# Weights-stationary products of a hybrid decoder layer: a pair of 512 and 256 columns, or three of 256 into one sum

## Chip, cores and metric

The kernel runs on one core of one Trainium2 chip. The metric is the device time of one execution in microseconds (us). Most of the computation is matrix products on TensorE (PE); VectorE (DVE), ScalarE (ACT) and GpSimd (POOL) prepare weights and finish results; SyncE (SP) issues the transfers of the weights. In the profile PEld is TensorE's loading of a stationary operand, which has rows of its own.

## What is computed

One decoder layer in float32 on 256 tokens of width 2048: a combined input projection into attention heads and a causal pooling mixer, an output projection into the residual, then a gated MLP of width 5632 with a causal convolution of width 3.

```python
D_MODEL, SEQ, D_FF, POOL_WINDOWS = 2048, 256, 5632, (2, 4, 8, 16)

def multiscale_pool(p, pool_w, pool_scale):     # 4 groups of 256 channels
    ...
        mixed = (cg[:, 1:] - cg[:, start]) / count - pf[:, :, sl]
        outs.append(jnp.einsum('bsc,cd->bsd', mixed.astype(p.dtype), pool_w[g]))
    ...

def conv_ffn(h, w_up, conv_w, conv_b, w_down):
    u = h @ w_up
    ...                                          # y = conv_b + sum of conv_w[i] * u shifted
    gate, val = jnp.split(y, 2, axis=-1)
    return (jax.nn.silu(gate) * val) @ w_down

def reference(x, ...):
    h = rms_norm(x, attn_norm_g[l])
    q, k, v, p = jnp.split(h @ w_in[l], ...)
    a = moba_attention(rms_norm(q), rms_norm(k), v, rel_bias)
    m = multiscale_pool(p, pool_w[l], pool_scale[l])
    x = x + jnp.concatenate([a, m], axis=-1) @ w_out[l]
    x = x + conv_ffn(rms_norm(x, ffn_norm_g[l]), w_up[l], conv_w[l], conv_b[l], w_down[l])
```

## The kernel before

**Split numbers.** To multiply float32 numbers with single-pass products, every operand is kept as two parts, a rounded one and the remainder. Weights arrive as `raw` chunks of 128x2048; ACT writes the rounded part `wh` (L115), DVE the remainder `wl` (L116). Activations (`xh`, `cat`, `x2h`, `hid`) are stored with both parts side by side, `[128, 16, 2, 256]`: for each of 16 slices of the inner dimension 256 tokens of the rounded part (index 0), then 256 of the remainder (index 1). A product is the sum of three terms: wh with part 0, wh with part 1, wl with part 0.

**Two kinds of product.** For q, k and v (`tok_half`, L145) the activations are stationary and 512 columns of weights move. For everything else (`feat_half`) a 128x128 block of weights is stationary and the tokens move: the pooling input, the output projection, the MLP's gate and value, the MLP's down projection. There `feat_mm` takes for each slice a **pair**: one product of wh with all 512 columns (both parts, L152), and one of wl with 256 columns (L154) that adds to the second half of the same PSUM tile. So a PSUM tile holds two halves, and `add_halves` (L379 on ACT, L380 on DVE) joins them in SBUF before anything else is done. The last block of the down projection and the pooling weights use `feat_sum` (L161) instead: three products of 256 columns into one sum, without halves to be joined.

**Blocks and queues.** A step is half a chunk of weights, 16 products in pairs for two output tiles; four steps (two chunks) make a block of 256 output channels in the MLP's up projection. Gate and value blocks alternate, in three groups of 8, 8 and 6, each followed by eight down blocks. After a block's last product, `gate` and `value` call `conv`: join the halves, times the row's scale into `u` (L561), three taps of the convolution into `y` (L566 on ACT, L567 and L569 on DVE), and for a value block the gate (L583) and the split into `hid` (L584, L585). `add_to_x2` does the same for the residual (L515). The order on each engine is that of the code: at every second step the next chunk but one is split, and its ACT and DVE instructions stand behind those of the block that ended before. There are three buffers for the two parts of weights, two for the PSUM tile `acc`.

**Pooling.** `pool_window` scales a group's channels by the row's scale into `pa[0]` (L386), adds shifted copies (L390), and leaves `pst` (L392, L393), on POOL for groups 3, 2 and 1 and on DVE for group 0; `pool_mixed` splits `pst` into `cat` (L399, L400).

**Places.** `WOFF` sets at which element each part of weights begins in a tile that is 64 elements longer than needed. The tiles of weights begin 32 bytes past a multiple of 256, those of the activations 128 bytes past one. From chunk 24 on (all weights-stationary chunks), wh begins at element 8, that is at 64 past a multiple of 256 and so 192 past the activations' place, counted round 256; wl begins at element 28, at 144 and so 16 past it. All slices and blocks that a product reads begin at multiples of 512 or 1024 bytes from there, so these distances hold for every one.

Of the kernel before, what the change touches and what calls it, by code (L numbers as in the profile page):

```python
# [23 lines left out]
F32 = mybir.dt.float32  # L24
F32R = mybir.dt.float32r
AF = mybir.ActivationFunctionType
OP = mybir.AluOpType
AX = mybir.AxisListType

P = 128  # L30
D = 2048
S = 256
# [16 lines left out]
NPAR = C_CB + 2 * NF  # L49
OK = (0, 4, 12, 8)  # L50
TOK_CHUNKS = 24
WOFF = ((24, 24), (8, 28))
THIRDS = ((0, 8), (8, 16), (16, 22))


# [16 lines left out]
def layer(ctx: ExitStack, tc: tile.TileContext, xT, wts, par, relT, ident_d, onehot_d, icnt_d, out):  # L72
    nc = tc.nc
# [3 lines left out]
    mm = ctx.enter_context(tc.tile_pool(name="mm", bufs=2, space=bass.MemoryType.PSUM))  # L77
# [5 lines left out]
    def acc(name):  # L83
        return mm.tile([P, 2, 512], F32, name=name, tag="acc")
# [4 lines left out]
    def small(name):  # L89
        return sm.tile([P, 512], F32, name=name, tag="small")  # L90
# [3 lines left out]
    def col(c):  # L94
        return pv[:, c:c + 1]
# [11 lines left out]
    def split_piece(c, lo, n):  # L107

        if c not in wparts:
            offs = WOFF[0 if c < TOK_CHUNKS else 1]  # L110
            wparts[c] = tuple(wpool.tile([P, CH + 64], F32R, name=w, tag=w)[:, o:o + CH]
# [15 lines left out]
    def half(u):  # L127

        parts = wparts[u // 2] if u % 2 == 0 else wparts.pop(u // 2)
        return tuple(w[:, (u % 2) * HALF:(u % 2 + 1) * HALF] for w in parts)  # L130
# [15 lines left out]
                                     start=(first and k == 0 and n == 0),  # L146
                                     stop=(last and k == 1 and n == 2))

    def feat_mm(ps, wh, wl, act, ks, first, last):

        for n, (ws, k) in enumerate(ks):
            nc.tensor.matmul(ps, wh[:, ws], act[:, k, :, :],  # L152
                             start=(first and n == 0), stop=False, skip_group_check=True)
            nc.tensor.matmul(ps[:, S:], wl[:, ws], act[:, k, 0, :], start=False,  # L154
                             stop=(last and n == len(ks) - 1), skip_group_check=True)

    def feat_sum(ps, wh, wl, act, ks, first, last):

        for n, (ws, k) in enumerate(ks):
            for i, (w, a) in enumerate(((wh, 0), (wh, 1), (wl, 0))):  # L160
                nc.tensor.matmul(ps, w[:, ws], act[:, k, a, :], start=(first and n == 0 and i == 0),  # L161
                                 stop=(last and n == len(ks) - 1 and i == 2))

    def feat_half(u, act, k0, ps, first, last, mm=feat_mm):
        wh, wl = half(u)
        for m in range(2):
            mm(ps[m], wh, wl, act,
               [(slice(k * 256 + m * P, k * 256 + (m + 1) * P), k0 + k) for k in range(4)],
               first, last)


    xh = keep.tile([P, KT, 2, S], F32R, name="xh", tag="h")
# [20 lines left out]
    ps = small("ps_start")  # L193
# [74 lines left out]
    rrow = keep.tile([P, S], F32, name="rrow", tag="rrow")  # L268
# [103 lines left out]
    PAD = 16  # L372
    pa = [early.tile([P, 2, PAD + S], F32, name=f"pa{i}") for i in range(3)]
    for t_ in pa:
        nc.gpsimd.memset(t_[:, :, :PAD], 0.0)

    def add_halves(dst, ps):

        nc.scalar.activation(dst, ps[:, :, S:], AF.Copy)  # L379
        nc.vector.tensor_tensor(dst, ps[:, :, :S], dst, op=OP.add)  # L380

    def pool_window(ps, g):
        s = early.tile([P, 2, S], F32, name="pst", tag=("sq", "hn")[g % 2])
        eng = nc.gpsimd if g else nc.vector
        add_halves(s, ps)
        eng.tensor_tensor(pa[0][:, :, PAD:], s, rrow[:, None, :].to_broadcast([P, 2, S]), op=OP.mult)  # L386
        cur, d, i = pa[0], 1, 1
        while d < WINDOWS[g]:
            nxt = pa[i]
            eng.tensor_tensor(nxt[:, :, PAD:], cur[:, :, PAD:], cur[:, :, PAD - d:PAD + S - d], op=OP.add)  # L390
            cur, d, i = nxt, 2 * d, 3 - i
        eng.tensor_tensor(s, cur[:, :, PAD:], icnt[:, g:g + 1, :].to_broadcast([P, 2, S]), op=OP.mult)  # L392
        eng.tensor_tensor(s, s, pa[0][:, :, PAD:], op=OP.subtract)  # L393
        st["win", g] = s
# [46 lines left out]
    def feat_block(act, ks, post, final=False):  # L441
        box, runs = {}, []
        for i, k0 in enumerate(ks):
            def run(u, i=i, k0=k0):
                if i == 0:
                    box["acc"] = None if final else acc("ps_feat")
                    box["ps"] = [small("ps_feat")[:, :S] if final else box["acc"][:, m, :] for m in range(2)]
                feat_half(u, act(), k0, box["ps"], i == 0, i == len(ks) - 1, feat_sum if final else feat_mm)
                if i == len(ks) - 1:
                    post(box["ps"] if final else box["acc"])  # L450
            runs.append([run])
        return runs
# [12 lines left out]
    for g in (3, 2, 1, 0):  # L465
        steps += feat_block(lambda: xh, XK, lambda ps, g=g: pool_window(ps, g))
        after(len(steps) + (2 if g else 0), lambda g=g: pool_mixed(g))
# [15 lines left out]
    for b in range(2):  # L483
# [4 lines left out]
        for j in range(4):  # L488
            h, u = 4 * b + j, at + 2 * j
# [8 lines left out]
    late = {}  # L498
# [11 lines left out]
            nc.gpsimd.memset(u[:, :, :2], 0.0)  # L510

    def add_to_x2(ps, g):
        x2, s = late["x2"][:, 2 * g:2 * g + 2, :], late["pool"].tile([P, 2, S], F32, name="fs", tag="fs", bufs=2)
        add_halves(s, ps)
        nc.vector.tensor_tensor(x2, s, x2, op=OP.add)  # L515
        return x2

    def residual(ps, g):
        x2 = add_to_x2(ps, g)
        if g == 0:  # L520
            nc.scalar.activation(late["sq"], x2, AF.Square)
            return
        s = late["pool"].tile([P, 2, S], F32, name="xs", tag="y0", bufs=2)
        nc.scalar.activation(s, x2, AF.Square)
        nc.gpsimd.tensor_tensor(late["sq"], late["sq"], s, op=OP.add)
# [30 lines left out]
    def conv(ps, f0_, which):  # L556

        pool, u = late["pool"], late["u"][which]
        s = pool.tile([P, 2, S], F32, name="fs", tag="fs", bufs=2)
        add_halves(s, ps)  # L560
        nc.vector.tensor_tensor(u[:, :, 2:], s, late["rrow"][:, None, :].to_broadcast([P, 2, S]), op=OP.mult)  # L561
        y = pool.tile([P, 2, S], F32, name="y", tag=f"y{which}", bufs=2)
        for m in range(2):
            f = f0_ + m
            cw = [col(C_CW + i * 2 * NF + f) for i in range(3)]
            nc.scalar.activation(y[:, m, :], u[:, m, 2:], AF.Identity, scale=cw[2], bias=col(C_CB + f))  # L566
            nc.vector.scalar_tensor_tensor(y[:, m, :], u[:, m, 1:1 + S], cw[1], y[:, m, :],  # L567
                                           op0=OP.mult, op1=OP.add)
            nc.vector.scalar_tensor_tensor(y[:, m, :], u[:, m, :S], cw[0], y[:, m, :],  # L569
                                           op0=OP.mult, op1=OP.add)  # L570
        return y

    def gate(ps, g):
        y = conv(ps, 2 * g, 0)
        nc.scalar.activation(y, y, AF.Silu)
        late["gate"] = y

    def value(ps, g, j):
        if j == 0:
            late["hid"] = keep.tile([P, KT, 2, S], F32R, name="hid", tag="c")  # L580
        y = conv(ps, NF + 2 * g, 1)
        hid, ks = late["hid"], slice(2 * j, 2 * j + 2)
        nc.vector.tensor_tensor(y, y, late["gate"], op=OP.mult)  # L583
        nc.scalar.activation(hid[:, ks, 0, :], y, AF.Copy)  # L584
        nc.vector.tensor_tensor(hid[:, ks, 1, :], y, hid[:, ks, 0, :].bitcast(F32), op=OP.subtract)  # L585

    def down(ps, g, last, final):
        x2 = late["x2"]
        if final:
            for m in range(2):  # L590
                k = 2 * g + m
                nc.vector.tensor_tensor(x2[:, k, :], ps[m], x2[:, k, :], op=OP.add)
                nc.sync.dma_start(out[:, k, :], x2[:, k, :])
            return
        add_to_x2(ps, g)
        if last:
            nc.sync.dma_start(out[:, 2 * g:2 * g + 2, :], x2[:, 2 * g:2 * g + 2, :])

    for n, (g0, g1) in enumerate(THIRDS):
# [4 lines left out]
        for g in range(D // 256):  # L604
            final = n == 2 and g == D // 256 - 1
            blocks.append(feat_block(lambda: late["hid"], range(0, 2 * (g1 - g0), 4),
                                     lambda ps, g=g, n=n, final=final: down(ps, g, n == 2, final), final))
# [4 lines left out]
    n = len(steps)  # L612
# [77 lines left out]
```

## Time and profile before

| | |
|---|---|
| median of 3 executions | 1046.59 us (1043.42 to 1058.9) |
| the profiled execution | 1045.45 us, its span 1043.3 us |
| PE busy | 1029.2 us, 5786 products |
| DVE, ACT busy | 690.5 us, 514.1 us |
| products as pairs (L152, L154) | 2472 of each |
| products in threes (L161) | 120 |
| joining halves (L379, L380) | 79 each |

The span reaches from the first instruction to the last of the profiled execution; 2.15 us lie around it. PE's rows overlap, since a product's row begins before the one ahead of it has ended; how fast products follow each other is read from the distance of their starts, not from their durations. In the sections below "pace" is that distance.

### The profile page before, as it was taken

Reading aid. Unit: us, or ns where it says so; the run is one execution under the profiler, and the core shown is the slowest. Engines: PE = TensorE matmul, PEld = TensorE weight load, DVE = VectorE, ACT = ScalarE, POOL = GpSimd, SP = SyncE. Lnnn points to the kernel's source line nnn. Section 1 sums busy time; section 2 is a strip of 40 time slices with the busy share of each in tenths; the row PEclk is TensorE's granted clock in tenths of the full one; section 3 lists DMA queues with packets and bytes.
Section 4 is the critical chain, followed back from the end, with each engine's and each line's share of the span. In section 5 each row is a group of like instructions: output and inputs, shape, how many; then the busy total and the mean of one; then the engine's idle time right before and its main releaser. Section 6 shows DMA issues by size and latency. Waiting matters only on the chain.

```text
span 1043.3 us, 13818 instructions
## 1 busy us (share of the span) xinstructions
PE 1029.2 (99%) x5786; PEld 894.1 (86%) x5786; DVE 690.5 (66%) x729; ACT 514.1 (49%) x532; POOL 63.2 (6%) x44
## 2 busy tenths in 40 slices
PE   9999999999999999999999999999999999999998
PEld 7788788888888888888888888888888888888887
DVE  6744667766567777777655677767765557777763
ACT  7534444546465455445433455455453344554541
POOL 0700004611110000000000000000000000000000
PEclk9999999999999999999999999999999999999999
DMA  9767644464644554454645444544565545545561
GB/s 342 271 169 205 226 171 161 152 245 182 225 166 161 190 212 164 185 217 163 239 173 199 186 173 167 211 188 162 206 221 196 184 161 202 203 161 182 218 205 41
DMA packets 31390, 200.42 MB, mean 192 GB/s; under 512 B 3816, under 2 KB 4872, under 8 KB 8544
## 3 DMA queue, kind: packets, MB, share of 16 engines
q1 hardware_dynamic: 30336, 196.92, 51.6%
q0 software_dynamic: 992, 2.63, 1.6%
q8 instruction: 45, 0.74, 0.3%
q14 instruction: 17, 0.14, 0.0%
HBM read 195.86 MB, written 3.67 MB: 191 GB/s over the span
## 4 chain that ended last, share of the span: by engine, by line
PE 55%; DVE 20%; ACT 10%; issue 8%; POOL 4%; DMA 3%; SPq 0%; ACTq 0%; DVEq 0%; POOLq 0%
PE ps_feat L152 31%; PE ps_feat L154 16%; DVE wl L116 8%; ACT wh L115 7%; PE ps_tok L145 6%; DMA raw<-in_wts 3%; DVE y L569 3%; DVE y L567 2%; DVE u L561 2%; DVE fs L380 2%; ACT y L566 2%; POOL xboth L274 1%; POOL pa L390 1%; DVE y L583 1%; PE ps_feat L161 1%
## 5 line engine op out<-in xcount | busy, mean ns | idle before, releaser
L116 DVE TENSOR_TENSOR wl<-raw,wh 128x2048 fp32r<-128x2048 f32 (+2 forms) x189 | 420.7, 2247 | 206.1 <-ACT wh L115 206.0
L152 PE MATMUL ps_feat<-x2h,wh 128*128 128x512 f32 x1408 | 488.8, 393 | 0.0
L154 PE MATMUL ps_feat<-x2h,wl 128*128 128x256 f32 x1408 | 391.9, 278 | 1.3 <-DVE wl L116 0.9
L115 ACT ACTIVATE wh<-raw 128x2048 fp32r<-128x2048 f32 (+2 forms) x189 | 342.9, 1837 | 96.1 <-PE ps_feat L152 58.4
L152 PEld LDWEIGHTS ps_feat<-x2h,wh 128*128 128x128 f32 x1408 | 263.9, 187 | 60.2
L154 PEld LDWEIGHTS ps_feat<-x2h,wl 128*128 128x128 f32 x1408 | 264.4, 188 | 4.8 <-DVE wl L116 4.4
L152 PE MATMUL ps_feat<-hid,wh 128*128 128x512 f32 x680 | 232.4, 390 | 0.0
L154 PE MATMUL ps_feat<-hid,wl 128*128 128x256 f32 x680 | 188.0, 277 | 0.5 <-DVE wl L116 0.5
L152 PEld LDWEIGHTS ps_feat<-hid,wh 128*128 128x128 f32 x680 | 127.6, 188 | 27.3
L154 PEld LDWEIGHTS ps_feat<-hid,wl 128*128 128x128 f32 x680 | 127.7, 188 | 0.8 <-DVE wl L116 0.8
L145 PE MATMUL ps_tok<-wh,xh 128*128 128x512 f32 x384 | 125.3, 402 | 0.5 <-ACT wh L115 0.5
L379 ACT ACTIVATE fs<-ps_feat 128x512 f32<-128x512 f32 x75 | 44.9, 599 | 131.5 <-PE ps_feat L154 131.5
L566 ACT ACTIVATE y<-u,pv 128x256 f32<-128x256 f32 x88 | 48.2, 595 | 116.7 <-DVE u L561 116.7
L145 PEld LDWEIGHTS ps_tok<-wh,xh 128*128 128x128 f32 x384 | 73.9, 192 | 16.5 <-ACT wh L115 0.7
L152 PE MATMUL ps_feat<-cat,wh 128*128 128x512 f32 x256 | 87.2, 389 | 0.0
L380 DVE TENSOR_TENSOR fs<-ps_feat,fs 128x512 f32<-128x512 f32 x75 | 51.5, 686 | 47.1 <-ACT fs L379 47.1
L145 PE MATMUL ps_tok<-wl,xh 128*128 128x512 f32 x192 | 76.4, 398 | 0.0
L154 PE MATMUL ps_feat<-cat,wl 128*128 128x256 f32 x256 | 70.7, 276 | 0.0
L567 DVE SCALAR_TENSOR_TENSOR y<-u,pv,y 128x256 f32<-128x256 f32 x88 | 42.4, 482 | 29.6 <-ACT y L566 29.6
L152 PEld LDWEIGHTS ps_feat<-cat,wh 128*128 128x128 f32 x256 | 48.1, 188 | 10.0
L154 PEld LDWEIGHTS ps_feat<-cat,wl 128*128 128x128 f32 x256 | 48.1, 188 | 0.0
L152 PE MATMUL ps_feat<-xh,wh 128*128 128x512 f32 x128 | 46.2, 403 | 0.0
(112 smaller groups left out, 568.6 us busy)
## 6 DMA issues: line engine op xcount, KB each, us to landing
raw<-in_wts SPq DMA_DIRECT2D x177, 1024.0 KB, 5.0
raw<-in_wts SPq DMA_DIRECT2D x6, 512.0 KB, 8.0
x<-in_xT SPq DMA_DIRECT2D x1, 2048.0 KB, 9.1
out<-x SPq DMA_DIRECT2D x7, 256.0 KB, 2.1
xboth<-in_xT SPq DMA_DIRECT2D x6, 256.0 KB, 7.9
band<-rsb POOLq DMA_DIRECT2D x1, 1536.0 KB, 37.2
raw<-in_wts SPq DMA_DIRECT2D x4, 256.0 KB, 4.1
T<-band POOLq DMA_DIRECT2D x2, 512.0 KB, 7.2
```

The lines of the kernel that those rows point to most:

```text
L115: nc.scalar.activation(wh, w, AF.Copy)
L116: nc.vector.tensor_tensor(wl, w, wh.bitcast(F32), op=OP.subtract)
L145: nc.tensor.matmul(ps[:, t, :], act[:, k0 + k, a, ts], w[:, ws], start=(first and k == 0 and n == 0), stop=(last and k == 1 and n == 2))
L152: nc.tensor.matmul(ps, wh[:, ws], act[:, k, :, :], start=(first and n == 0), stop=False, skip_group_check=True)
L154: nc.tensor.matmul(ps[:, S:], wl[:, ws], act[:, k, 0, :], start=False, stop=(last and n == len(ks) - 1), skip_group_check=True)
L161: nc.tensor.matmul(ps, w[:, ws], act[:, k, a, :], start=(first and n == 0 and i == 0), stop=(last and n == len(ks) - 1 and i == 2))
L379: nc.scalar.activation(dst, ps[:, :, S:], AF.Copy)
L380: nc.vector.tensor_tensor(dst, ps[:, :, :S], dst, op=OP.add)
L561: nc.vector.tensor_tensor(u[:, :, 2:], s, late["rrow"][:, None, :].to_broadcast([P, 2, S]), op=OP.mult)
L566: nc.scalar.activation(y[:, m, :], u[:, m, 2:], AF.Identity, scale=cw[2], bias=col(C_CB + f))
L567: nc.vector.scalar_tensor_tensor(y[:, m, :], u[:, m, 1:1 + S], cw[1], y[:, m, :], op0=OP.mult, op1=OP.add)
L569: nc.vector.scalar_tensor_tensor(y[:, m, :], u[:, m, :S], cw[0], y[:, m, :], op0=OP.mult, op1=OP.add)
```

## The change

Every weights-stationary product uses `feat_sum`; `feat_mm` and `add_halves` go; what used the joined halves reads PSUM directly. wl begins at element 8 like wh, so both are 192 bytes past the activations' place.

```diff
-WOFF = ((24, 24), (8, 28))
+WOFF = ((24, 24), (8, 8))
...
-    def feat_mm(ps, wh, wl, act, ks, first, last):
-        for n, (ws, k) in enumerate(ks):
-            nc.tensor.matmul(ps, wh[:, ws], act[:, k, :, :],
-                             start=(first and n == 0), stop=False, skip_group_check=True)
-            nc.tensor.matmul(ps[:, S:], wl[:, ws], act[:, k, 0, :], start=False,
-                             stop=(last and n == len(ks) - 1), skip_group_check=True)
...
     def feat_sum(ps, wh, wl, act, ks, first, last):
         for n, (ws, k) in enumerate(ks):
             for i, (w, a) in enumerate(((wh, 0), (wh, 1), (wl, 0))):
                 nc.tensor.matmul(ps, w[:, ws], act[:, k, a, :], start=(first and n == 0 and i == 0),
                                  stop=(last and n == len(ks) - 1 and i == 2))
...
-    def add_halves(dst, ps):
-        nc.scalar.activation(dst, ps[:, :, S:], AF.Copy)
-        nc.vector.tensor_tensor(dst, ps[:, :, :S], dst, op=OP.add)
...
     def pool_window(ps, g):
         eng = nc.gpsimd if g else nc.vector
-        add_halves(s, ps)
-        eng.tensor_tensor(pa[0][:, :, PAD:], s, rrow[:, None, :].to_broadcast([P, 2, S]), op=OP.mult)
+        nc.vector.tensor_tensor(pa[0][:, :, PAD:], ps, rrow[:, None, :].to_broadcast([P, 2, S]), op=OP.mult)
...
     def add_to_x2(ps, g):
-        x2, s = late["x2"][:, 2 * g:2 * g + 2, :], late["pool"].tile([P, 2, S], F32, name="fs", tag="fs", bufs=2)
-        add_halves(s, ps)
-        nc.vector.tensor_tensor(x2, s, x2, op=OP.add)
+        x2 = late["x2"][:, 2 * g:2 * g + 2, :]
+        nc.vector.tensor_tensor(x2, ps, x2, op=OP.add)
...
     def conv(ps, f0_, which):
-        s = pool.tile([P, 2, S], F32, name="fs", tag="fs", bufs=2)
-        add_halves(s, ps)
-        nc.vector.tensor_tensor(u[:, :, 2:], s, late["rrow"][:, None, :].to_broadcast([P, 2, S]), op=OP.mult)
+        nc.vector.tensor_tensor(u[:, :, 2:], ps, late["rrow"][:, None, :].to_broadcast([P, 2, S]), op=OP.mult)
```

On PE, at the first slices of the first gate block, there stands before:

```order
L152 MATMUL ps_feat<-x2h,wh 128x512
L154 MATMUL ps_feat<-x2h,wl 128x256
L152 MATMUL ps_feat<-x2h,wh 128x512
L154 MATMUL ps_feat<-x2h,wl 128x256
L152 MATMUL ps_feat<-x2h,wh 128x512
L154 MATMUL ps_feat<-x2h,wl 128x256
```

and now, where L153 is `feat_sum` and "x2" means twice in a row:

```order
L153 MATMUL ps_feat<-x2h,wh 128x256 x2
L153 MATMUL ps_feat<-x2h,wl 128x256
L153 MATMUL ps_feat<-x2h,wh 128x256 x2
L153 MATMUL ps_feat<-x2h,wl 128x256
L153 MATMUL ps_feat<-x2h,wh 128x256 x2
L153 MATMUL ps_feat<-x2h,wl 128x256
```

A slice moves 768 columns as before, in three products instead of two, and each of the three has a weight load of its own.

On DVE, at the end of the first gate block and the splits behind it, there stands before (u is the scaled result, y the convolution):

```order
L380 TENSOR_TENSOR fs<-ps_feat,fs 128x512
L561 TENSOR_TENSOR u_1739<-fs,rrow_2468 128x2x256
L567 SCALAR_TENSOR_TENSOR y<-u_1739,pv,y 128x256
L569 SCALAR_TENSOR_TENSOR y<-u_1739,pv,y 128x256
L567 SCALAR_TENSOR_TENSOR y<-u_1739,pv,y 128x256
L569 SCALAR_TENSOR_TENSOR y<-u_1739,pv,y 128x256
L116 TENSOR_TENSOR wl<-raw,wh 128x2048 x2
```

and now:

```order
L544 TENSOR_TENSOR u_1875<-ps_feat,rrow_2844 128x2x256
L550 SCALAR_TENSOR_TENSOR y<-u_1875,pv,y 128x256
L552 SCALAR_TENSOR_TENSOR y<-u_1875,pv,y 128x256
L550 SCALAR_TENSOR_TENSOR y<-u_1875,pv,y 128x256
L552 SCALAR_TENSOR_TENSOR y<-u_1875,pv,y 128x256
L116 TENSOR_TENSOR wl<-raw,wh 128x2048 x2
```

One DVE instruction of each block is gone, with the copy on ACT that it waited for; the others keep their order.

More of the change, by code (lines that the diff above doesn't have):

```diff
@@ L162, in feat_sum, with feat_half @@
                                  stop=(last and n == len(ks) - 1 and i == 2))
-    def feat_half(u, act, k0, ps, first, last, mm=feat_mm):
+    def feat_half(u, act, k0, ps, first, last):
         wh, wl = half(u)
         for m in range(2):
-            mm(ps[m], wh, wl, act,
-               [(slice(k * 256 + m * P, k * 256 + (m + 1) * P), k0 + k) for k in range(4)],
-               first, last)
+            feat_sum(ps[m], wh, wl, act,
+                     [(slice(k * 256 + m * P, k * 256 + (m + 1) * P), k0 + k) for k in range(4)],
+                     first, last)
     xh = keep.tile([P, KT, 2, S], F32R, name="xh", tag="h")
@@ L445, in run @@
                 if i == 0:
-                    box["acc"] = None if final else acc("ps_feat")
+                    box["acc"] = None if final else acc("ps_feat")[:, :, :S]
                     box["ps"] = [small("ps_feat")[:, :S] if final else box["acc"][:, m, :] for m in range(2)]
-                feat_half(u, act(), k0, box["ps"], i == 0, i == len(ks) - 1, feat_sum if final else feat_mm)
+                feat_half(u, act(), k0, box["ps"], i == 0, i == len(ks) - 1)
                 if i == len(ks) - 1:
```

## The prediction

> **What bounds the kernel now.** First the page's span, its busy times and the chain that ended last.
>
> ```profile
> span 1043.3 us, 13818 instructions
> PE 1029.2 (99%) x5786; PEld 894.1 (86%) x5786; DVE 690.5 (66%) x729; ACT 514.1 (49%) x532; POOL 63.2 (6%) x44
> PE 55%; DVE 20%; ACT 10%; issue 8%; POOL 4%; DMA 3%; SPq 0%; ACTq 0%; DVEq 0%; POOLq 0%
> ```
>
> PE is hardly ever idle; DVE and ACT have a third and a half to spare, but stand in the chain with 30%. So the change is worth what it does to the pace of PE's products, and to the waits that DVE and ACT cause. Next, where the products lie, from the view of line L152, and a mean by tile, from the page's groups.
>
> ```profile
> L152 PE MATMUL ps_feat<-x2h,wh x1408: 388/390/579, 305.6 to 973.0; 128*128 128x512 f32 x176
> L152 PE MATMUL ps_feat<-hid,wh x680: 388/389/399, 485.8 to 1030.5; 128*128 128x512 f32 x170
> L152 PE MATMUL ps_feat<-x2h,wh 128*128 128x512 f32 x1408 | 488.8, 393 | 0.0
> L152 PE MATMUL ps_feat<-hid,wh 128*128 128x512 f32 x680 | 232.4, 390 | 0.0
> L152 PE MATMUL ps_feat<-cat,wh 128*128 128x512 f32 x256 | 87.2, 389 | 0.0
> ```
>
> The MLP's 2088 pairs fill the stretch from 305.6 to 1030.9 (where the first product in threes starts, below): 725.3 us, 347.4 ns a pair. The timeline of PE shows that this is no uniform pace. Two stretches, first columns start and duration:
>
> ```profile
> 500.22 0.39 PE L152 MATMUL ps_feat<-hid,wh 128*128 128x512 f32 x1
> 500.45 0.28 PE L154 MATMUL ps_feat<-hid,wl 128*128 128x256 f32 x1
> 500.56 0.39 PE L152 MATMUL ps_feat<-hid,wh 128*128 128x512 f32 x1
> ...
> 501.24 0.39 PE L152 MATMUL ps_feat<-hid,wh 128*128 128x512 f32 x1
> ```
>
> ```profile
> 344.65 0.40 PE L152 MATMUL ps_feat<-x2h,wh 128*128 128x512 f32 x1
> 344.88 0.28 PE L154 MATMUL ps_feat<-x2h,wl 128*128 128x256 f32 x1
> ...
> 346.06 0.40 PE L152 MATMUL ps_feat<-x2h,wh 128*128 128x512 f32 x1
> ```
>
> Three pairs from 500.22 to 501.24 are 340 ns each; four from 344.65 to 346.06 are 353. The instructions are the same, no wait lies between, and the granted clock (the column behind the five engines' busy times) is full in both:
>
> ```profile
> 344.00:346.00 2.00, 2.00 (x13) 1.71 (x13) 1.22 (x3) 0.71 (x2) 0.00 (x0) 1.00 0.92 365
> 500.00:502.00 2.00, 2.00 (x14) 1.76 (x13) 1.53 (x1) 0.00 (x0) 0.00 (x0) 1.00 1.00 406
> ```
>
> So a pair has two paces, about 340 and 354 (13 or 14 ns apart). L152's durations tell the shares: 0.39 at the one, 0.40 at the other, in the view of the line 388 to 389 against some 397; a mean of 393 over x2h is half of 1408, 390 over hid an eighth of 680, 389 over cat none. That makes about 790 pairs times 14 ns, 11 us; with 5 us of waits (below) it accounts for 725.3 minus 2088 times 340, that is 15.4 us.
>
> **What three products cost.** The last block already runs in threes, with wl still at 16:
>
> ```profile
> 1030.55 0.39 PE L152 MATMUL ps_feat<-hid,wh 128*128 128x512 f32 x1
> 1030.78 0.28 PE L154 MATMUL ps_feat<-hid,wl 128*128 128x256 f32 x1
> 1030.89 0.39 PE L161 MATMUL ps_feat<-hid,wh 128*128 128x256 f32 x2
> 1031.12 0.28 PE L161 MATMUL ps_feat<-hid,wl 128*128 128x256 f32 x1
> 1031.24 0.40 PE L161 MATMUL ps_feat<-hid,wh 128*128 128x256 f32 x2
> ...
> 1039.02 0.40 PE L161 MATMUL ps_feat<-hid,wh 128*128 128x256 f32 x2
> ```
>
> From 1030.89 to 1039.02 are 23 threes: 353.5 ns each. With this number for all, the change loses. But look at the first three, entered from a stretch at 340: the two products of wh take 0.23 together, 0.115 each, the product of wl 0.12, and the next three 0.35. A weight load runs beside the product ahead of its own, and in a pair the load of wh, at 192, runs beside the 256 columns of wl: 500.45 to 500.56 is 0.11, the good pace. Only in threes does wl, at 16, load beside 256 columns. I read this so: a load at 192 beside 256 columns costs nothing at the good pace, one at 16 disturbs it, and from then on all run at 118. With both parts at 192 every product repeats what wh has shown, so **I take 113.3 ns, 340 for three**. From below, half the clock gives a bound: in the pooling stage PE runs at 0.50 for a while,
>
> ```profile
> 215.00:217.50 2.50, 2.50 (x13) 2.50 (x13) 2.43 (x4) 0.61 (x2) 0.00 (x0) 0.50 0.00 0
> 215.00 0.63 PE L161 MATMUL ps_pool<-cat,wh 128*128 128x256 f32 x2
> 217.56 0.60 PE L161 MATMUL ps_pool<-cat,wh 128*128 128x256 f32 x2
> ```
>
> twelve products from 215.00 to 217.56, 213 ns each; at the full clock that would be 107, 320 for three. From above, three products that each take the 0.12 to 0.125 of a wl product are 366. Both ends are kept for the range.
>
> The Trainium skill, page "TensorE: Matmul & The Clock Gate", section "Step-by-step: what each phase is for", says that loading the next weights takes no read bandwidth from the running product, since each has a port of its own. By that rule the place of wl changes nothing and three products stay where the last block has them; that is the first rival below. The trace speaks against it in part: one pair, at one clock, has two paces. The same page, section "Back-to-back issue gap", gives 256/2.4 + 2.5, about 109 ns a product, 327.5 for three (an estimate from that page); the sum would then be some 31 us better. No stretch here shows 109.
>
> **Terms.** Product pace in the MLP: 2088 times 340 is 709.9, against 725.3 minus 5 of waits, that is **10 us** saved; the 256 pairs on cat stand at 340 already, the 128 on xh and the 24 last threes (13.5 ns each, 0.3 us) give about **1**.
>
> Waits for split weights. The view of waits, and the turn of DVE and ACT before one of them:
>
> ```profile
> PEld ps_feat L154 <- DVE wl L116: 5.2, 11, 0.8
> 328.04 0.60 ACT L379 ACTIVATE fs<-ps_feat 128x512 f32<-128x512 f32 x1 [1.13 <-PE ps_feat L154]
> 329.54 0.68 DVE L380 TENSOR_TENSOR fs<-ps_feat,fs 128x512 f32<-128x512 f32 x1
> 330.26 0.69 DVE L561 TENSOR_TENSOR u<-fs,rrow 128x512 f32<-128x512 f32 x1
> ...
> 334.84 3.72 ACT L115 ACTIVATE wh<-raw 128x2048 fp32r<-128x2048 f32 x2
> 336.78 4.50 DVE L116 TENSOR_TENSOR wl<-raw,wh 128x2048 fp32r<-128x2048 f32 x2 [1.12 <-ACT wh L115]
> 339.13 0.19 PEld L154 LDWEIGHTS ps_feat<-x2h,wl 128*128 128x128 f32 x1 [0.33 <-DVE wl L116]
> ```
>
> After a value block ACT cannot split weights until DVE has the convolution and gate done. That chain holds L379 (0.60) and L380 (0.68); both go. L561 reads PSUM in their stead; L380 reads PSUM too and takes 0.68 against L561's 0.69, so that costs nothing (it lies on DVE beside PE's products in any case). 1.3 us less in a chain whose waits are 0.8 at most: I count **4 of the 5 us** as gone. What is late next is PE itself. DVE now waits for PE's last product where it waited for ACT's copy; behind it stand the next two wl splits, and these are due one block (32 threes of 340 ns, 10.9 us) later.
>
> Pooling. Before the pooling products PE waits for DVE's join of group 0, which stands behind POOL's window of group 1:
>
> ```profile
> 201.80 1.29 POOL L386 TENSOR_TENSOR pa<-pst,rrow 128x512 f32<-128x512 f32 x1 [3.49 <-DVE pst L380]
> 210.67 1.30 POOL L393 TENSOR_TENSOR pst<-pst,pa 128x512 f32<-128x512 f32 x1
> 214.01 0.50 PE L161 MATMUL ps_pool<-cat,wh 128*128 128x256 f32 x2 [2.05 <-DVE pst L380]
> ```
>
> Scaling moves to DVE, in the place of the join, so POOL's chain loses its 1.29 and PE's wait of 2.05 shrinks to some 0.7. The half clock quoted above follows this wait; the twelve products and a few ahead and behind lose 0.1 us each there, 2 us at most, which may go or stay. I take **2**, between 1.3 and 3.3. The new hazard is that DVE overwrites `pa[0]`, which POOL reads to the end of the group ahead: with POOL done at 211.97 for group 1, and DVE's L400 waiting for the same end already, it adds no wait.
>
> Sum: 10 + 1 + 4 + 2 = 17 us. I give back 2, since any wait may set off a stretch at 118 again (the one at 339 is followed by one). 1045.45, the profiled execution (1043.3 of span and 2.15 around it, 1.1 below the median), becomes **1030**.
>
> **Rivals.** (1) Placement does nothing, threes stay at 353.5. 2088 times 353.5 is 738.1, 12.8 above 725.3; cat adds 256 times 13.5, 3.5, xh 1; pooling gives 2 back: 1061, slower than before. It decides if a load at 192 beside 256 columns keeps the pace only because the one ahead of it was beside 512. For it: in the last block wh's products, too, run at 0.115 to 0.12. Chance 0.17. (2) Both paces remain, as now, half and half: 1045, no change. For it: x2h has spells at 353 with wh at 192. Chance 0.17. (3) A load at 192 frees the array altogether, towards 320: half the way, 330, is 25 us less than the forecast, 1005; DVE's and ACT's turn (328.04 to 339.13 above, less 1.3, some 10 us a block) would then begin to bind. Against it: no product of 256 columns in a stretch without waits falls below 0.11. Chance 0.10. (4) A load at 192 beside every product disturbs each like wl's: 366 for three, 2472 times 19 is 47 above now, 1090. Chance 0.06. The forecast keeps 0.50.
>
> **Range and chances.** The forecast's own range is 1023 (all waits and the half clock gone, every three at 340) to 1037 (some spells at 118, pooling unchanged). With (1) and (2), 1022 to 1064 leaves out 0.16 and tails. A change of 2%, some 21 us, is about what a measurement of this kernel can tell from none: faster needs less than 1026, which is (3) and a fifth to a quarter of the forecast, 0.22; slower needs over 1067, (4) and the tail of (1), 0.08; the rest 0.70.
>
> **What would show it.** PE's starts three products apart: 340, 354 or both. The waits of PEld for wl near 1 us instead of 5.2. The span's stretch for the MLP near 711 us. DVE's busy time lower by 79 times 0.69 less three scalings taken over from POOL, about 52, ACT's by 47, with no effect of their own. Clock 1.00 through the pooling stage, or another dip. I am wrong if the pace depends on something other than where wl lies, above all if 118 is simply what a weight load for every 256 columns costs.

## The result, and the profile after

| | before | after |
|---|---|---|
| median of 20 executions | 1054.08 us | 1057.34 us |
| lowest | 1043.42 us | 1055.22 us |
| profiled execution | 1045.45 us | 1055.83 us |

The ratio after to before is 1.0069, 95% interval 1.0043 to 1.0094: slower by 0.7%, where 1030 us was forecast. Ratios here and below are taken over the executions within 1.5% of the fastest of the same kernel. From the page of after, its span, its busy times and the chain by engine:

```profile
span 1054.0 us, 18605 instructions
PE 1042.7 (99%) x8258; PEld 1015.2 (96%) x8258; DVE 640.3 (61%) x653; ACT 469.5 (45%) x453; POOL 55.1 (5%) x41
PE 92%; DMA 3%; ACT 1%; POOL 1%; DVE 1%; issue 0%; SPq 0%; DVEq 0%; ACTq 0%
```

DVE and ACT have left the chain (20% and 10% before, 1% each now), and PE alone is late. The timeline of PE, start and duration, from the second stretch that was shown of before:

```profile
499.93 0.40 PE L153 MATMUL ps_feat<-hid,wh 128*128 128x256 f32 x2
...
501.34 0.40 PE L153 MATMUL ps_feat<-hid,wh 128*128 128x256 f32 x2
```

Four threes in 1.41 us, 353 ns each. It is so from the products on cat to the end, which windows show: length, busy time and count of PE, PEld, DVE, ACT and POOL (below, for other kernels, of PE alone), granted clock, DMA share, GB/s.

```profile
215.00:217.50 2.50, 2.50 (x23) 2.50 (x23) 1.62 (x1) 1.26 (x3) 0.00 (x0) 1.00 0.66 279
320.00:480.00 160.00, 160.00 (x1361) 160.00 (x1360) 108.82 (x113) 77.44 (x73) 0.00 (x0) 1.00 0.49 185
760.00:1040.00 280.00, 280.00 (x2380) 280.00 (x2379) 162.60 (x138) 114.45 (x87) 0.00 (x0) 1.00 0.49 179
```

A count takes in about two products that reach in from ahead, so a pace is the length by the count less two: 160 by 1359 is 117.7 ns, to the end. (In windows of some 20 us this is good to half a per cent.) The half clock of the pooling stage is gone: 1.00 where before had 0.50. Where the time lies, from the view of the line after (durations in ns, first and last start in us), then three rows of before:

```profile
L153 PE MATMUL ps_feat<-x2h,wh x2816: 279/280/467, 303.4 to 982.0; 128*128 128x256 f32 x188
L153 PE MATMUL ps_feat<-hid,wl x704: 279/279/279, 485.0 to 1049.9; 128*128 128x256 f32 x176
L153 PE MATMUL ps_feat<-cat,wh x512: 279/280/280, 207.3 to 303.2; 128*128 128x256 f32 x171
L153 PE MATMUL ps_pool<-cat,wh x32: 279/280/280, 210.1 to 218.4; 128*128 128x256 f32 x32
```

```profile
L152 PE MATMUL ps_feat<-cat,wh x256: 388/389/398, 209.1 to 305.3; 128*128 128x512 f32 x128
L161 PE MATMUL ps_pool<-cat,wh x32: 277/281/416, 214.0 to 223.8; 128*128 128x256 f32 x32
L161 PE MATMUL ps_feat<-hid,wl x24: 278/280/286, 1031.1 to 1039.2; 128*128 128x256 f32 x24
```

The MLP took 305.6 to 1039.2, 733.6 us, and takes 303.4 to 1049.9, 746.5: 12.9 more. From the first product on cat to the last wh of pooling it was 14.7 us and is 11.1: 3.6 less. Ahead of cat stand 1.8 us less, behind the pooling products, on cat, 3.2 more. Together 10.7, as the spans say.

### The profile page after: what moved, and what is told of

Read it like the earlier page. It is cut to its first block, busy times and chain, and to the rows that moved or that the text cites. A ratio compares the mean times of both kernels' runs of the same rounds, so it can differ in the third digit from the quotient of the medians.

```text
span 1054.0 us, 18605 instructions
## 1 busy us (share of the span) xinstructions
PE 1042.7 (99%) x8258; PEld 1015.2 (96%) x8258; DVE 640.3 (61%) x653; ACT 469.5 (45%) x453; POOL 55.1 (5%) x41
## 4 chain that ended last, share of the span: by engine, by line
PE 92%; DMA 3%; ACT 1%; POOL 1%; DVE 1%; issue 0%; SPq 0%; DVEq 0%; ACTq 0%
PE ps_feat L153 84%; PE ps_tok L145 6%; DMA raw<-in_wts 3%; POOL xboth L266 1%; ACT wh L115 1%; DVE wl L116 1%; PE ps_pool L153 1%; PE ps_s L323 0%; PE ps_av L355 0%; PE ps_T L310 0%; PE ps_eT L345 0%; DVE xh L180 0%; ACT xboth L263 0%; SPq L174 0%; ACT xh L179 0%
## 5 line engine op out<-in xcount | busy, mean ns | idle before, releaser
L153 PE MATMUL ps_feat<-x2h,wh 128*128 128x256 f32 x2816 | 497.9, 280 | 0.0
L153 PEld LDWEIGHTS ps_feat<-x2h,wh 128*128 128x128 f32 x2816 | 429.9, 188 | 0.1
L153 PE MATMUL ps_feat<-x2h,wl 128*128 128x256 f32 x1408 | 392.8, 279 | 0.0
L153 PEld LDWEIGHTS ps_feat<-x2h,wl 128*128 128x128 f32 x1408 | 263.3, 187 | 0.0
L153 PE MATMUL ps_feat<-hid,wh 128*128 128x256 f32 x1408 | 248.9, 280 | 0.0
L153 PEld LDWEIGHTS ps_feat<-hid,wh 128*128 128x128 f32 x1408 | 214.8, 188 | 0.0
L153 PE MATMUL ps_feat<-hid,wl 128*128 128x256 f32 x704 | 196.4, 279 | 0.0
L153 PEld LDWEIGHTS ps_feat<-hid,wl 128*128 128x128 f32 x704 | 131.6, 187 | 0.0
L153 PE MATMUL ps_feat<-cat,wh 128*128 128x256 f32 x512 | 90.6, 280 | 0.0
L153 PEld LDWEIGHTS ps_feat<-cat,wh 128*128 128x128 f32 x512 | 78.2, 188 | 0.0
L153 PE MATMUL ps_feat<-cat,wl 128*128 128x256 f32 x256 | 71.4, 279 | 0.0
L544 DVE TENSOR_TENSOR u<-ps_feat,rrow 128x512 f32<-128x512 f32 x44 | 30.4, 692 | 30.2 <-PE ps_feat L153 30.0
L153 PEld LDWEIGHTS ps_feat<-cat,wl 128*128 128x128 f32 x256 | 47.9, 187 | 0.0
L500 DVE TENSOR_TENSOR x<-ps_feat,x 128x512 f32<-128x512 f32 x31 | 21.4, 690 | 42.2 <-PE ps_feat L153 36.6
L153 PE MATMUL ps_feat<-xh,wh 128*128 128x256 f32 x256 | 46.8, 284 | 0.0
```

Of the source, the lines that this page charges most:

```text
L500: nc.vector.tensor_tensor(x2, ps, x2, op=OP.add)
L544: nc.vector.tensor_tensor(u[:, :, 2:], ps, late["rrow"][:, None, :].to_broadcast([P, 2, S]), op=OP.mult)
```

## Experiments

**The two parts of the change apart.** The threes, with wl left at 16:

```diff
-WOFF = ((24, 24), (8, 8))
+WOFF = ((24, 24), (8, 28))
```

> The changed kernel with wl back at 16 past the activations' place; the change of place alone is undone. Place theory as predicted: slower than the changed kernel, threes over 353 ns, 1060 us or more. Load theory: threes at 353 as with both at 192, 1057. Rhythm theory: the same 353, or 340 in some stretches, 1030 to 1057.

1057.36 us, ratio 1.0042 (1.0002 to 1.0082). By windows of PE:

```profile
320.00:480.00 160.00, 160.00 (x1361) 1.00 0.49 185
```

The count is that of after: moving wl from 16 to 192 changed nothing. The other part, the pairs of before with wl at 192:

```diff
-WOFF = ((24, 24), (8, 28))
+WOFF = ((24, 24), (8, 8))
```

> The kernel before (pairs of 512 and 256 columns, halves joined) with wl at 192 past the activations' place like wh; nothing else is changed. Place theory: a load at 192 never disturbs the moving columns, so all pairs run at 340 ns instead of partly at 354, and the time is 1030 to 1036 us. Load theory (118 ns is what a weight load for every 256 columns costs, wherever the weights lie): the pairs, with a load for every 384 columns, don't care, time and paces as before, 1045 to 1059. Rhythm theory (the moving columns have two paces, and which one holds is set by how an earlier wait shifted loads against products): both paces as before, 1045 to 1059.

1062.51 us, ratio 1.0111 (1.0054 to 1.0169).

```profile
320.00:480.00 160.00, 160.00 (x907) 1.00 0.49 183
```

Some 453 pairs in 160 us, 353 ns each, and none of the MLP at 340: each part by itself gives the slow pace throughout. That goes against the prediction's reading, by which wl at 16 was the disturber: with every load at 192 the pairs lost the stretches at 340 that they had with wl at 16. Then the changed kernel with the old finish given back, by a copy on ACT and a maximum on DVE:

```diff
+    def through_sbuf(dst, ps):
+        nc.scalar.activation(dst, ps, AF.Copy)
+        nc.vector.tensor_tensor(dst, ps, dst, op=OP.max)
...
+        through_sbuf(s, ps)                  # in add_to_x2 and in conv
```

> The changed kernel, both parts at 192, but in the residual and in the convolution the sum goes through SBUF as before the change: a copy on ACT, then a DVE instruction that reads PSUM and the copy (their maximum, which is the sum itself), then the old instruction. That gives DVE and ACT their old chain back, with threes. Lock theory: waits of PE for wl come back, 3 to 6 us in all, and with them chances to change the pace: stretches at 340 and at 353, 1045 to 1062. If waits don't change the pace: all at 353, and the waits on top, 1060 to 1063.

1057.76 us, ratio 1.0075 (1.0039 to 1.0112).

```profile
320.00:480.00 160.00, 160.00 (x1361) 1.00 0.48 182
```

The same count again: at 353 a three DVE and ACT have time for the old chain too, no load in the MLP waits for wl, and reading PSUM directly is worth nothing as long as PE is this slow.

**Place or entry.** An entry is what stands directly ahead of a stretch of like products: a wait, another place of the weights, another kind of product. To part it from the place, the changed kernel walks through 16 places, four chunks (64 threes) at each. The place is 16 bytes times (i - 6), counted round 256, for group i from chunk 24 on:

```diff
-            offs = WOFF[0 if c < TOK_CHUNKS else 1]
+            offs = WOFF[0] if c < TOK_CHUNKS else ((c - TOK_CHUNKS) // 4 % 16 * 4,) * 2
```

> The changed kernel with another place for both parts of the weights in every four chunks: 16 places in steps of 16 bytes, round 256 bytes, each two or three times. Place theory: the pace of three products changes from group to group by place, between 340 and 366 ns, the same at both times that a place comes. Load theory: 353 at every place. Rhythm theory: 340 or 353, without relation to the place.

Windows in groups at 192, 64, 80 and 192:

```profile
209.50:231.50 22.00, 22.00 (x189) 1.00 0.70 278
391.50:413.00 21.50, 21.50 (x192) 1.00 0.52 196
413.50:435.50 22.00, 22.00 (x188) 1.00 0.51 193
572.80:594.20 21.40, 21.40 (x191) 1.00 0.51 193
```

192 and 64 can run at 113 a product, with three products and a load for each; 192 did so in this window at 572.8 and in a third at 934.9 (189 in 21.1 us), but not in the one at 209.5 (117.6). In the other groups I found 116.6 to 120. So the forecast's pace exists at the forecast's place, and the place alone does not bring it. The same places in falling order:

```diff
+            offs = WOFF[0] if c < TOK_CHUNKS else (-((c - TOK_CHUNKS) // 4) % 16 * 4,) * 2
```

> The run over 16 places again, with the places in falling order, so that each is entered from the one above it instead of the one below. Place theory: the same pace at each place as in rising order (340 at 64, 116 to 120 a product elsewhere). Lock theory: most places keep their pace, but 192 and 64 can come out at 340 or at 353, by the entry.

Windows at 192, 64 and 192:

```profile
483.00:504.00 21.00, 21.00 (x180) 1.00 0.53 198
665.50:686.50 21.00, 21.00 (x188) 1.00 0.51 201
846.00:867.00 21.00, 21.00 (x181) 1.00 0.54 196
```

64 has the good pace from this side too; 192, entered from the other side, has 118 both times. The other places come out alike in both directions and at each visit, to half a nanosecond: 116.7 at 208 and 120 at 0 for example; of the 16, only 192 and 64 showed more than one pace.

Next, the width: in the gate and value blocks 128, 384 and 512 columns move in the three groups of blocks. Columns are left out or summed twice there; the down blocks are as in the changed kernel.

```diff
+            for i, w in enumerate((wh, wh, wl)):
+                c = 512 if start else cols
+                nc.tensor.matmul(ps[:, :c], w[:, ws], moving[:, :c], start=start, ...)
```

> The changed kernel with other widths of the moving columns in the gate and value blocks, each product with its weight load: 128 columns in the first group of such blocks, 384 in the second, 512 in the third (the first product of each sum is 512 wide; the first group leaves out half of the tokens' terms, the others add columns that don't belong to the sum). Load theory: 118 ns at 128 columns, since the load sets the pace; 170 at 384 and 227 at 512, the good pace. Rhythm theory: 384 columns at 170 or 177, 512 at 227 or 236, and 128 columns at 57 to 59, or at some 107 if the load binds, not 118. Place theory: 177 and 236, or 170 and 227, by whether 192 is a good place, and 128 columns below 118.

Windows: 128 columns, the down blocks behind them, the down blocks behind 384 columns, and 512 columns:

```profile
330.00:430.00 100.00, 100.00 (x878) 1.00 0.51 193
520.00:560.00 40.00, 40.00 (x356) 1.00 0.51 185
840.00:910.00 70.00, 70.00 (x597) 1.00 0.54 195
950.00:1050.00 100.00, 100.00 (x438) 1.00 0.27 95
```

The first row, 114 a product, holds the first products of the sums, which are 512 wide; between those, products of 128 columns follow at 111.7. So half the columns take 111.7 where 256 take 113 or 118: something beside the columns holds a product of 128 back. Whether that is its load no run shows. And the same down products, at 192 both times, ran at 113 behind one stage and at 118 behind the next.

One chunk in sixteen at 176 as a kick:

```diff
+            offs = WOFF[0] if c < TOK_CHUNKS else ((4, 4) if (c - TOK_CHUNKS) % 16 == 0 else (8, 8))
```

> The changed kernel, but every 16th chunk of the weights-stationary part (chunk 24, 40 and so on) lies at 176 instead of 192 past the activations' place; all others stay at 192. Lock theory: the change of place throws the rhythm over, and some or all of the ten stretches that follow run at 340, as two of three did in the run over 16 places; 1031 to 1048 us. Stage theory: 192 goes on at 353 as in the changed kernel, 1057.

1057.97 us, ratio 1.0092 (1.0064 to 1.0120); 117.7 throughout, against the lock theory's 1031 to 1048 us:

```profile
320.00:480.00 160.00, 160.00 (x1361) 1.00 0.49 184
```

**64 throughout, and where it is lost.** `WOFF = ((24, 24), (40, 40))`.

> The changed kernel with both parts of the weights at 64 past the activations' place instead of 192. In the run over 16 places the threes ran at 340 ns there both times. Lock theory (two paces hold themselves, and how a stretch is entered decides which): if 64 holds only the good one, all threes at 340 and 1029 to 1034 us; if it holds both, 353 from some point on and up to 1057. Stage theory (the place is good or bad by what else goes on in that part of the program): paces change by stage, 1040 to 1057.

1053.69 us, ratio 1.0043 (1.0008 to 1.0077). Windows, then the timeline between them:

```profile
240.00:307.00 67.00, 67.00 (x594) 1.00 0.55 200
311.00:480.00 169.00, 169.00 (x1437) 1.00 0.49 182
```

```profile
307.43 0.28 PE L153 MATMUL ps_feat<-x2h,wl 128*128 128x256 f32 x1
307.55 0.39 PE L153 MATMUL ps_feat<-x2h,wh 128*128 128x256 f32 x2
307.77 0.28 PE L153 MATMUL ps_feat<-x2h,wl 128*128 128x256 f32 x1
307.89 0.59 PE L251 MATMUL ps_row<-sq,ones 128*128 128x256 f32 x2
308.13 0.59 PE L153 MATMUL ps_feat<-x2h,wh 128*128 128x256 f32 x2
308.55 0.28 PE L153 MATMUL ps_feat<-x2h,wl 128*128 128x256 f32 x1
...
308.90 0.28 PE L153 MATMUL ps_feat<-x2h,wl 128*128 128x256 f32 x1
```

The out-projection and the first threes of the MLP run at 113.3 (340 from 307.43 to 307.77). At 307.89 stands the row product of the MLP's scale, in float32 (two rows). From the wl product ahead of it to the next are 0.78, one three and some 0.44 for the row product; the three behind that takes 0.35, and PE stays at 117.8. No row has a wait.

**Entering again behind the row product.** Chunks 52 to 55 at 80, all others at 64:

```diff
+            offs = WOFF[0] if c < TOK_CHUNKS else ((44, 44) if 52 <= c < 56 else (40, 40))
```

> All parts of weights 64 past the activations' place, but chunks 52 to 55, the first after the row product at the start of the MLP, 48 past... that is element 44 in place of 40 (80 past). Theory A (a place has two paces and keeps the one it is entered with; 64 is entered at the good one by a change of place): the out-projection runs at 113.3 a product, the stretch behind the row product at 117.7 to 120, and from chunk 56 (about 330 us) to the end at 113.3, since nothing interrupts PE there: about 1960 threes at 340 in place of 353, so some 26 us less than with 64 throughout, about 1026 us, faster than before by 2 to 3%. Theory B (the good stretch of 64 is a matter of the stage, not of the entry): 117.7 from chunk 56 too, 1053 us as with 64 throughout. If the pace falls back at some product of the MLP, the trace shows where.

1026.43, 1028.17 and 1026.13 us; ratio 0.9789 (0.9715 to 0.9862) for these three. A fourth execution took 1057.46, the time of 117.7 throughout; it has no trace. Windows in the four chunks and in the last quarter:

```profile
316.00:338.00 22.00, 22.00 (x188) 1.00 0.45 169
760.00:1012.00 252.00, 252.00 (x2226) 1.00 0.51 186
```

118.3 in the four chunks, 113.3 at the end, and so from about 341 us on. So theory A holds, at its 1026, in three executions of four. With PE at 340 no load in the MLP waits for wl, where before had 5.2 us of such waits; the one wait in the weights-stationary part, 0.2 us, stands at 235.6, in the out-projection. The same with one chunk, 52, at 48:

```diff
+            offs = WOFF[0] if c < TOK_CHUNKS else ((36, 36) if c == 52 else (40, 40))
```

> As the kernel ahead, but the change of place is one chunk (52, 16 threes) and from the other side: element 36 in place of 40, 48 past the activations' place. Theory A: one change is enough, 113.3 from chunk 53 to the end, about 1025 us. Rival: a switch needs a longer stretch or the other direction (one chunk of sixteen at 176 did not switch the kernel with 192): 117.7 throughout, 1053 us.

1030.32, 1054.74, 1028.16, 1053.34 us: by their times two executions switched and two did not. The profiled one, the first, did, behind the chunk:

```profile
335.00:480.00 145.00, 145.00 (x1281) 1.00 0.50 191
```

The same entry for the forecast's place, chunks 52 to 55 at 176 and the rest at 192, `(4, 4)` and `(8, 8)`:

> The changed kernel, both parts at 192, but chunks 52 to 55 (behind the row product at the start of the MLP) at element 4, 176 past the activations' place, as the good stretches of the kernel that walks through the places were entered. Theory A (192 has both paces, and the prediction's sum fails only in the entry): 113.3 from chunk 56, about 340 us, to the end: 1054 less 27, about 1027 us. Rival: 192 takes the good pace from below two times in three only, so some executions at 1027 and some at 1054. Rival: 192 is not held by this entry at all: 1055 us.

1057.67 us (1056.01 to 1059.49), ratio 1.0064 (1.0029 to 1.0099); theory A's forecast failed here.

```profile
345.00:480.00 135.00, 135.00 (x1148) 1.00 0.50 187
```

117.8. By their times all ten executions stayed there: 192 holds the good pace when it has it (for 80 us in the down blocks behind 128 columns), but this entry does not give it. Nor does another, the products of three steps (111, 175 and 239) taken as two of 128 columns each:

```diff
+                if pace["kick"]:
+                    for t in range(NT):
+                        ts = slice(t * P, (t + 1) * P)
+                        nc.tensor.matmul(ps[:, ts], w[:, ws], act[:, k, a, ts], start=False, ...)
+                    continue
```

> The changed kernel at 192, but in three steps of the MLP (111, 175, 239, about 345, 525 and 710 us) each product of 256 columns is taken as two of 128 columns, nothing left out. Theory A, with what the kernel of several widths showed (behind 128-column products, which follow at some 111, the threes at 192 ran at 113.3): 117.7 up to the first such step, 113.3 behind it, with 24 products more a step (some 2.5 us each, 8 in all): 1054 less 25 plus 8, about 1035 us. Rival: it was the stage's length or its different sums, and 117.7 stays: about 1062 us.

1065.17 us, ratio 1.0155 (1.0089 to 1.0220): the rival's 1062 and a little more.

```profile
355.00:480.00 125.00, 125.00 (x1064) 1.00 0.48 180
```

Three entries at 64, `(44, 44) if c // 4 in (13, 15, 21) else (40, 40)`:

> 64 throughout, with chunks 52 to 55, 60 to 63 and 84 to 87 at element 44. With one such entry three executions of four came to 1026 to 1028 us and one to 1057. If each entry succeeds three times in four by itself, a failed one is mended at 60 or 84, and the good pace is kept where it stood: each entry costs 64 threes at 119 in place of 113.3 a product, 1.1 us, so 1028 to 1030 us, rarely up to 1040, never 1055. If instead an execution is good or bad as a whole (by something set at its start), some executions stay at 1055 or more.

1035.04 us: five executions from 1032.67 to 1035.69, ratio 0.9838 (0.9787 to 0.9890), and one of 1051.55, without a trace. Windows behind the first, the second and the third entry:

```profile
341.00:361.00 20.00, 20.00 (x179) 1.00 0.52 195
390.00:510.00 120.00, 120.00 (x1021) 1.00 0.51 193
523.00:680.00 157.00, 157.00 (x1388) 1.00 0.51 188
```

113, then 117.8, then 113.3: the second entry lost what the first had given, and the third brought it back. So in this execution it was decided at each entry, not once for all, and an entry is a risk where the pace is good already. My 1028 to 1030 had not counted that.

**What ends the good pace.** The kernel with one entry, and two float32 row products more:

```diff
+    def row_again():
+        nc.tensor.matmul(small("ps_row")[:, :S], ones, late["sq"][:, 0, :], start=True, stop=True)
+    for u in (138, 234):
+        after(u, row_again)
```

> As the first kernel of this call, with two more row products (one float32 product of the squares each, read by nothing, waiting for nothing) behind steps 138 and 234, about 410 and 685 us. Theory A: if the good pace holds from chunk 56 on, the row product itself ends it, as it does at 307.89 us in the trace of 64 throughout: 113.3 up to about 410 us, 117.7 from there to the end, about 1047 us. Rival: at 307.89 it was the wait or POOL's and DVE's work at this place; the added products cost 0.3 us each and the pace stays at 113.3, about 1027 us.

1054.18 us, above theory A's 1047 in part because the out-projection had lost the good pace already (below). The first added product stands at about 417 us:

```profile
345.00:416.00 71.00, 71.00 (x629) 1.00 0.51 192
425.00:680.00 255.00, 255.00 (x2167) 1.00 0.51 190
```

113.2 up to it, 117.8 behind. The same with single-pass products of rounded numbers (`wr` is a rounded copy of `ones`, x2h moves):

```diff
+        nc.tensor.matmul(small("ps_row")[:, :S], late["wr"][:, :P], late["h"][:, 0, 0, :], start=True, stop=True)
```

> The kernel with the two added row products (behind steps 138 and 234), but these are single-pass products of 256 rounded numbers, as all around them, with a stationary operand of their own; the one at the start of the MLP stays float32. If it is the float32 product (several passes) that ends the good pace: 113.3 from chunk 56 to the end, about 1027 us. If any product with another place or another PSUM tile does it: 117.7 from about 410 us, 1054 us, as with the float32 ones.

1027.19 us. Its timeline at the first, and the window behind:

```profile
414.60 0.28 PE L541 MATMUL ps_row<-x2h,wr 128*128 128x256 f32 x1
414.71 0.40 PE L153 MATMUL ps_feat<-x2h,wh 128*128 128x256 f32 x2
414.95 0.28 PE L153 MATMUL ps_feat<-x2h,wl 128*128 128x256 f32 x1
```

```profile
420.00:670.00 250.00, 250.00 (x2208) 1.00 0.52 194
```

Around the foreign product the distances are 0.11 to 0.12 (its neighbours' 0.40 shows the disturbance), and behind it 113.3 is back. Last, 64 throughout with the real row product in a single pass:

```diff
+        sr = late["pool"].tile([P, S], F32R, name="sr")
+        nc.scalar.activation(sr, sq[:, 0, :], AF.Copy)
+        row_scale(late["rrow"], sr, late["pool"], late["wr"])
```

> 64 throughout, without any change of place, but the row product at the start of the MLP is a single-pass one of rounded squares (rounded by one more ACT instruction). If the float32 product ends the good pace: an execution that has it in the out-projection keeps it to the end, about 1020 to 1025 us; one that loses it at some 230 us, as two of the last call did, stays at 117.7, 1055 us. If any such break ends it: 117.7 from some 310 us in all, 1053 us.

Ten executions, median 1053.26 us; one took 1029.32, the others 1050.35 to 1054.48.

```profile
310.65 0.28 PE L153 MATMUL ps_feat<-x2h,wl 128*128 128x256 f32 x1
310.77 0.28 PE L251 MATMUL ps_row<-sr,wr 128*128 128x256 f32 x1
310.88 0.40 PE L153 MATMUL ps_feat<-x2h,wh 128*128 128x256 f32 x2
311.12 0.28 PE L153 MATMUL ps_feat<-x2h,wl 128*128 128x256 f32 x1
```

Here one foreign product of 0.11 us, without a wait, ended the good pace in the profiled execution (353 a three from 311.12 on). So it is not float32 alone: in every trace of 64 that reached a float32 row product at the good pace, that pace ended there, and a single-pass product may end it or not. (Here a tile of its own, sr, moves, where in the kernel ahead x2h did; whether that makes the difference was not tried.) A wait may end it too. At some 236 us, in the out-projection, PE stops shortly for wl: 64 throughout (0.23 us) and the kernel with one entry of four chunks (0.17) kept the good pace behind it, the one with two float32 row products more (0.18) lost it, and the one with one chunk lost it at a gap of 0.03.

## Why the prediction was wrong

**The failed step** is "I take 113.3 ns, 340 for three", taken from the reading that a load at 192 beside 256 columns costs nothing and one at 16 disturbs. The sum for the MLP was 2088 times 340, 10 us less than before without its waits. Measured: 746.5 us against 733.6 less 5.2 of waits, 18 us more, since every three took 353. The place of wl was not the disturber: threes run at 353 with wl at 16 as at 192, and pairs lost the good pace when wl went to 192. The first doubt at the prediction's end, that "the pace depends on something other than where wl lies", was right.

I read the good pace of wh at 192 as what the place does, and said in the same breath that "from then on all run at 118"; that second half was the finding. From the products on cat on, a stretch of threes keeps the pace that it was entered with: in all these traces it changes only at a change of place or of width, at a product of another kind, or at a short stop of PE. 192 allows the good pace but does not bring it. After was at the slow pace ahead of the products on cat (their durations are 280 already), and nothing later switched it. The unknown was the entry, and the sum had no term for it but 2 us "given back". That an entry changes the pace is shown at 64. At 192 the runs show both paces, but the entries made on purpose all failed, so that a better entry would have brought the changed kernel itself to 340 is argued, not shown.

**The terms beside it held.** The waits for wl went from 5.2 us to nothing, where 4 were counted. The runs divide the credit in part: at 353 they are gone with the old finish as well, and at 340 there are none in the MLP with the direct reading; threes at 340 with the old finish were not run, and the 5.2 are those of pairs at both paces. Pooling gave 3.6 where 2 was taken and 3.3 was the bound; the clock is 1.00 there. DVE's busy time fell by 50 and ACT's by 45 (52 and 47 forecast), with no effect of their own. What was named as late next, PE itself, is.

**Rival (1)** came nearest: its MLP, 12.8 more, was measured as 12.9. Its 1061 is 5 above the profiled 1055.83, since pooling gave 1.6 more than it took, and 3 us fell away ahead of the products on cat. Its reason was wrong: place does matter (113 at 64 and 192, 116.6 to 120 elsewhere). The rule of the Trainium skill, page "TensorE: Matmul & The Clock Gate", section "Step-by-step: what each phase is for", by which loading the next weights takes no read bandwidth from the running product, does not explain this. The runs that differ in place alone differ in pace; whether it is the load that makes the difference they do not show.

**The closing doubt**, that 118 "is simply what a weight load for every 256 columns costs", was wrong too: with a load for every 256 columns the threes ran at 113.3 for 680 us. Entered well, at 64, the threes come to 1026 to 1028 us, so the sum, 1030, is about right for a kernel that holds the pace.

**Before** has the same two paces, but its pairs change between them in another way. In its trace the first 65 blocks of the MLP, of 32 pairs each, run at one pace from their sixth pair on, 42 at 340 and 23 at 353, by the starts of L152; all 16 changes of pace stand at the start of a block, and at 12 of these the profile shows no wait. And the float32 row product, which ended the good pace in each trace of 64 that reached it at that pace, left it as it was in the pairs (340 a pair from 314.58 to 315.26):

```profile
313.81 0.59 PE L259 MATMUL ps_row<-sq,ones 128*128 128x256 f32 x2
...
314.58 0.39 PE L152 MATMUL ps_feat<-x2h,wh 128*128 128x512 f32 x1
...
315.26 0.39 PE L152 MATMUL ps_feat<-x2h,wh 128*128 128x512 f32 x1
```

So a pair does not simply keep the pace that it was entered with, and what the threes showed must not be carried over to pairs.

What stays open: what in the array or its reads holds the two paces; why an entry at 64 succeeds in most executions, and at 192 in the walk upwards through the places but in none that was made on purpose; what set the good pace of the down blocks behind the 128-column stage; and why pairs change pace at the start of a block, and never reach 340 in the MLP with wl at 192. Before's executions lie between 1042.51 and 1061.89 us, one of 2648.61 apart; that this spread comes from its paces is argued from its one trace, not shown for the others.

## What to carry to other kernels

Where the same instructions show two paces in one trace, without a wait between, look for the instruction at which the pace switches before reading a cause from what differs between two neighbouring rows; a place or a shape that was seen at the good pace is not yet shown to bring it. A pace that is held needs an entry, and a product of another kind or a short wait behind it may end it: here four chunks of weights at another place, some 9 us behind the last such product, were worth 25 us and more in three executions of four (1026 to 1028 against 1053.69 us), and a second entry put it at risk. Taking work off engines that are not late is worth at most what their waits were, 5 us here, and nothing while PE is so slow that it never has to wait.

## What the runs showed of the hardware

Threes of 256 columns, with a load for each product, have two paces, 113.3 and 117.7 ns a product, both at the granted clock of 1.00 and without waits, with hysteresis: hundreds of microseconds at either, and a switch within a few products. The rows' durations tell them apart, 276 ns against 280. Places of both parts of the weights 64 and 192 bytes past the activations', counted round 256, allow the good one; at the 14 others that were tried it did not occur, and each of those has a pace of its own, from 116.7 to 120. In pairs with wl at 16 the good one occurs as well, and comes and goes at the starts of blocks. A product of 128 columns with its load took 111.7 ns, only 1.6 less than one of 256 at the good pace; 512 with a load each took 229. A float32 product of 256 columns, which takes some 0.44 us, cost some 24 us by what it left behind: from 417 us to the end the threes of that kernel ran at 117.8 instead of 113.3. (The whole difference, 1054.18 against 1027.19 with single-pass products in its place, holds another 3 us of the out-projection, which had lost the good pace before.)
